# One layer of a streaming encoder: program order on every engine up to the MLP, the long convolution wholly on VectorE by a budget per weight unit, and w_out with twelve columns before the heads' rows

## The chip, the cores and the metric

One core of a Trainium2 chip runs the whole layer in one launch. The metric is the device time of an execution in microseconds (us), lower is better. TensorE (PE) multiplies, VectorE (DVE), ScalarE (ACT) and GpSimd (POOL) do the elementwise work, and the queue of SyncE (SP) issues nearly all transfers.

## What is computed

256 tokens of width 2048, float32. The layer is, cut to what matters:

```python
h = rms_norm(x, norm_mix_pre);  u = h @ w_in              # 2048 -> 4352 columns, split among three mixers
y_a = B * conv3(C * v)                                     # short convolution, 6 groups of 128 channels
y_b = silu(layer_norm(conv31(val * sigmoid(gate)) + bias)) # 6 heads of 128, norm over all 768 channels
y_c = (trailing_mean(u_c, {2,4,8,16}) - u_c) @ pool_w * pool_scale   # 4 groups of 128
x = x + rms_norm(concat(y_a, y_b, y_c) @ w_out, norm_mix_post)
h = rms_norm(x, norm_ffn_pre);  gate, val = split(conv3(h @ w_up) + bias)   # 2 x 5632 columns
x = x + rms_norm((silu(gate) * val) @ w_down, norm_ffn_post)
```

## The kernel before

**Units.** All four weight matrices lie in memory as one stream of units, each 128 partitions by 1024 floats (512 KB): units 0 to 67 are `w_in`, 68 to 99 `w_out`, 100 to 275 `w_up`, then `w_down`. A unit holds 8 blocks of 128 x 128. To reach float32 accuracy, every weight is split in a high and a low part: `load` (L97) brings `raw`, `split_hi` (L102) copies it rounded to `whi` on ScalarE, `split_lo` (L111) writes `wlo = raw - whi` on VectorE. There are 4 `raw` buffers and 5 of `whi` and `wlo`. The activations (`h1`, `y_t`, `h2`) are split the same way by `make_hi` (L332) and `make_lo` (L335). `product` (L244) runs three matmuls of 256 tokens for a block: `whi` with the high and the low activations, `wlo` with the high ones. So a unit is 24 matmuls. `ahead(u)` (L121) issues the splits up to unit u + 4 before the matmuls of unit u.

**First group.** `mm_group` (L284) takes the first 4 columns of `w_in` with 2 rows of blocks in a unit (units 0 to 7), while `start(k)` (L341) makes `h1` row by row from the loaded `xT` and squares it for the norm. GpSimd adds the squares.

**In-projection.** `mm_pair` (L276) makes two columns in 4 units, from unit 8 to 67: pairs for the 6 heads of mixer B (two of them in the first group), 2 pairs of pools, then `cv`, `cv`, `b` three times for mixer A. `evacuate` (L554) reads a finished pair from PSUM. For a head (`head_glu`, L390) it makes `glu`, and then the convolution with 31 taps: taps 2 to 22 are `tap` on VectorE (L404), in two sums `acc`; the last 8 (`POOL_TAPS`) are a ScalarE product `p` (L423) and a GpSimd add (L424) into `accp`, which GpSimd adds to `acc` at L427. The taps are closures in the list `background`. `between(kind)` pops 4 or 5 of them (`PACE`) in the middle and at the end of a pair. After the sixth head come the layer norm's closures: `mean`, six `centre`, `variance`, six `finish`. `later(n, f)` runs f some units later, at `tick`, after a unit's matmuls.

**w_out.** Its rows come in `OUT_ORDER`: pools, mixer A, then the heads (mixer B). The first 8 columns are one group, one row of blocks per unit (units 68 to 83). Before row 9 whatever is left of `background` is issued at once. Then the columns follow in pairs, the last pair (14, 15) in one PSUM tile `o14`; `out_tiles` (L591) squares and scales finished columns on ScalarE.

**The order on an engine.** Instructions of this part are issued through `nc.vector` and its like, and the framework's scheduler, which has its own time model, places them on each engine, except where `pin` keeps the program's order. `pinned` is False until the end of w_out, True from there to the norm of the MLP's input, and False again after it. Loads are pinned up to the end of the first group's section (L363). PSUM has 3 tiles of two banks (`banks`) and 2 small ones.

After w_out come a norm, `w_up` in pairs with a gate for each, `w_down` and the last norm.

## Time and profile before

| what | value |
|---|---|
| median of 3 runs | 1063.74 us (1062.91 to 1063.87) |
| the profiled execution | 1063.24 us |
| its span, first to last instruction | 1061.4 us |
| TensorE matmul busy | 1043.9 us, 98% of the span |
| VectorE, ScalarE, GpSimd busy | 730.0, 559.6, 194.3 us |
| granted TensorE clock, mean | 0.998 |
| read from memory | 194.57 MB, 185 GB/s over the span |

Busy time is time in which an engine executes; a wait of TensorE is a gap between its matmuls, put down to the instruction that ended it. Only gaps of the engine that sets the end cost anything. The first group runs to about 33 us, the in-projection to 213 us, w_out to 308 us, the MLP to the end.

### The profile page before, as it was taken

To read this page: it belongs to the slowest core of one execution; us is meant where nothing else is said; L and a number is where in the kernel's file an instruction comes from. 1 tells how busy PE (TensorE), PEld (TensorE's weight loads), DVE (VectorE), ACT (ScalarE), POOL (GpSimd) and SP (SyncE) were. 2 spreads that over 40 slices of the span, in tenths; PEclk is the share of its full clock that TensorE was granted. 3 is DMA by queue.
4 is the path that set the end of the run, shared out by engine and by line. 5 is a ranking of instruction groups with operands and counts; after the bars stand their busy time and mean duration, and the time that the engine had idled before them with its cause. 6 is when DMAs were issued, how large, how long until landed. Compare 5 with 4: busy or idle time off the path is not lost.

```text
span 1061.4 us, 16686 instructions
## 1 busy us (share of the span) xinstructions
PE 1043.9 (98%) x6485; PEld 932.1 (88%) x6485; DVE 730.0 (69%) x949; ACT 559.6 (53%) x781; POOL 194.3 (18%) x203
## 2 busy tenths in 40 slices
PE   8989999999999999999999999999999999999997
PEld 7989899999989988888888888888888888888886
DVE  7899988764448697786867868766766444454543
ACT  8645445556446575564655646655555343343431
POOL 4333556331114221110110101111111000000000
PEclk9999999999999999999999999999999999999999
DMA  8646466656645563765847648556556656565552
GB/s 278 221 139 193 156 188 201 202 174 186 193 139 178 181 192 124 233 204 151 251 153 225 213 133 261 188 192 191 186 186 232 188 189 195 183 193 184 195 180 80
DMA packets 73454, 199.85 MB, mean 188 GB/s; under 512 B 23712, under 2 KB 24608, under 8 KB 73248
## 3 DMA queue, kind: packets, MB, share of 16 engines
q1 hardware_dynamic: 72944, 197.39, 59.0%
q10 hardware_dynamic: 432, 1.40, 0.3%
q8 instruction: 51, 0.84, 0.3%
q14 instruction: 27, 0.22, 0.1%
HBM read 194.57 MB, written 2.10 MB: 185 GB/s over the span
## 4 chain that ended last, share of the span: by engine, by line
PE 89%; DVE 6%; issue 3%; DMA 1%; ACT 1%; SPq 0%; POOLq 0%; POOL 0%; DVEq 0%; ACTq 0%
PE gv L257 28%; PE gv L253 14%; PE o L247 9%; PE d L791 7%; PE d L793 7%; PE d L792 7%; PE in_cv L247 5%; PE up L247 4%; DVE acc L404 4%; PE in_b L247 3%; DVE wlo L115 1%; PE in L247 1%; DMA raw<-in_w_in 1%; PE in_head L247 1%; PE d3b L793 1%
## 5 line engine op out<-in xcount | busy, mean ns | idle before, releaser
L115 DVE TENSOR_TENSOR wlo<-raw,whi 128x1024 fp32r<-128x1024 f32 (+1 forms) x365 | 455.8, 1253 | 243.7 <-ACT whi L109 242.9
L109 ACT ACTIVATE whi<-raw 128x1024 fp32r<-128x1024 f32 (+1 forms) x365 | 383.9, 1055 | 334.5 <-PE d L793 103.1
L257 PE MATMUL gv<-h,whi 128*128 128x512 f32 x1280 | 443.2, 394 | 0.0
L253 PE MATMUL gv<-h,wlo 128*128 128x256 f32 x1280 | 346.3, 281 | 0.0
L257 PEld LDWEIGHTS gv<-h,whi 128*128 128x128 f32 x1280 | 234.9, 188 | 49.6
L253 PEld LDWEIGHTS gv<-h,wlo 128*128 128x128 f32 x1280 | 240.7, 188 | 6.8
L755 POOL TENSOR_TENSOR cg<-cg,cv 128x256 f32<-128x256 f32 x44 | 59.6, 1357 | 392.4 <-ACT cg L753 345.5
L791 PE MATMUL d<-whi,g_hi 128*128 128x512 f32 x308 | 121.7, 395 | 0.0
L793 PE MATMUL d<-whi,g_lo 128*128 128x512 f32 x308 | 121.2, 394 | 0.0
L792 PE MATMUL d<-wlo,g_hi 128*128 128x512 f32 x308 | 121.1, 393 | 0.0
L247 PE MATMUL o<-y_t,whi 128*128 128x256 f32 x512 | 91.5, 282 | 1.7 <-ACT yo L599 1.7
L247 PEld LDWEIGHTS o<-y_t,whi 128*128 128x128 f32 x512 | 78.5, 188 | 1.9 <-ACT yo L599 1.9
L247 PE MATMUL o<-y_t,wlo 128*128 128x256 f32 x256 | 72.0, 281 | 0.0
L793 PEld LDWEIGHTS d<-whi,g_lo 128*128 128x128 f32 x308 | 57.8, 188 | 13.9
L792 PEld LDWEIGHTS d<-wlo,g_hi 128*128 128x128 f32 x308 | 57.8, 188 | 13.6
L791 PEld LDWEIGHTS d<-whi,g_hi 128*128 128x128 f32 x308 | 57.8, 188 | 13.4
L247 PE MATMUL in_cv<-h,whi 128*128 128x256 f32 x384 | 68.9, 282 | 0.0
L404 DVE SCALAR_TENSOR_TENSOR acc<-glu,vec_sb,acc 128x246 f32<-128x246 f32 (+10 forms) x126 | 66.5, 567 | 2.5 <-POOL acc L427 2.2
L247 PEld LDWEIGHTS in_cv<-h,whi 128*128 128x128 f32 x384 | 59.0, 188 | 0.1
L247 PE MATMUL in_cv<-h,wlo 128*128 128x256 f32 x192 | 54.1, 282 | 1.1 <-DVE wlo L115 1.1
L749 ACT ACTIVATE u<-gv 128x512 f32<-128x512 f32 x40 | 23.7, 593 | 58.5 <-PE gv L257 58.5
L750 DVE TENSOR_TENSOR u<-gv,u 128x512 f32<-128x512 f32 x40 | 27.5, 688 | 37.8 <-ACT u L749 37.8
(155 smaller groups left out, 1275.2 us busy)
## 6 DMA issues: line engine op xcount, KB each, us to landing
raw<-in_w_up SPq DMA_DIRECT2D x176, 512.0 KB, 4.0
raw<-in_w_down SPq DMA_DIRECT2D x88, 512.0 KB, 3.5
raw<-in_w_in SPq DMA_DIRECT2D x67, 512.0 KB, 4.1
raw<-in_w_out SPq DMA_DIRECT2D x32, 512.0 KB, 4.1
xT<-blocks SPq DMA_DIRECT2D x64, 32.0 KB, 3.5
xT<-in_xt SPq DMA_DIRECT2D x7, 256.0 KB, 5.2
out<-tail_sb SPq DMA_DIRECT2D x6, 256.0 KB, 2.4
tail_sb<-in_g_row ACTq DMA_DIRECT2D x1, 1024.0 KB, 7.9
```

Of the source, the lines that this page charges most:

```text
L109: pin(nc.scalar.activation(hi[:, s], raws[i][:, s], AF.Copy))
L115: pin(nc.vector.tensor_tensor(lo[:, s], raw[:, s], hi[:, s].bitcast(F32), ALU.subtract))
L247: nc.tensor.matmul(ps, w, x, start=opens and n == 0, stop=last and n == 2, skip_group_check=True)
L253: pin(nc.tensor.matmul(ps[:, :T], w_lo, h[:, 0], start=False, stop=False))
L257: pin(nc.tensor.matmul(ps, w_hi, h, start=opens, stop=last))
L404: nc.vector.scalar_tensor_tensor(a[:, o:], glu[:, : T - o], cb(s), a[:, o:], ALU.mult, ALU.add)
L749: nc.scalar.activation(u, ps[:, :, T:], AF.Copy)
L750: nc.vector.tensor_tensor(u, ps[:, :, :T], u, ALU.add)
L755: nc.gpsimd.tensor_tensor(a, a, b, ALU.mult)
L791: nc.tensor.matmul(pss[h], g_hi[:, k, s], w1, start=(k == 0), stop=False)
L792: nc.tensor.matmul(pss[h], g_hi[:, k, s], w2, start=False, stop=False)
L793: nc.tensor.matmul(pss[h], g_lo[:, k, s], w1, start=False, stop=(k == KF - 1))
```

## The change

**Order.** `pinned` starts as True, and a wrapper `InOrder` pins whatever goes through `tensor`, `vector`, `scalar`, `gpsimd` in this part. Up to the MLP, every engine runs in the order in which the program issues. In the MLP the old `nc.` names remain.

**Start.** `step(n)` issues all of one unit's preparation: `make_hi`, `split_hi`, `make_lo`, `split_lo`, and the squares of the rows before. It runs four units ahead. Units 0 to 2 are split in halves and unit 1 is loaded in halves; row 1 of `xT` is loaded between the halves of unit 0; rows 8 to 13 no longer stand behind `raw` buffers in the queue, and unit 4's weights stand behind them.

**Budget.** `begin(u)` replaces `tick`, `between` and `PACE`. Ahead of the matmuls of unit u it runs what is due, then the splits (`ahead`), then the reading of a finished pair, then as many pieces of `background` as a credit allows: each unit adds 11.2 - 4.9 (in quarters of a microsecond), a tap costs 1.65, reading a pair 2.8 or 3.2, and so on.

**The convolution.** `POOL_TAPS` is gone: all taps from 2 to 30 of a head are VectorE instructions, 29 instead of 21. With them go the 48 ScalarE products, 42 GpSimd adds into `accp` and 6 GpSimd adds at L427. The head's sum for the norm is added when the head closes. Delays (`later`) are longer: 5 units to the mean's product, 3 to the variance's, 3 and 4 for the pools.

**w_out.** `OUT_TILES`: the ten rows of pools and mixer A for columns 0 to 7 and 8 to 11 (units 68 to 82), then the heads' six rows for 12 columns, 4 at a time (units 83 to 91), then columns 12 to 15 whole. Columns 14 and 15 have PSUM tiles of their own.

The number of matmuls, splits and loaded bytes is unchanged.

```diff
+FREE = 10
+OUT_TILES = (
+    [(k, m) for k in range(FREE) for m in range(8)]
+    + [(k, m) for k in range(FREE) for m in range(8, 12)]
+    + [(k, m) for g in (0, 4, 8) for k in range(FREE, KD) for m in range(g, g + 4)]
+    + [(k, m) for m in range(12, KD) for k in range(KD)]
+)
...
+SLOT, SPLIT, TAP = 11.2, 4.9, 1.65
+LOAD = {"head": 2.8, "pool": 3.2, "cv": 3.2, "b": 2.8}
...
     raws, parts = {}, {}
-    pinned, loading = [False], [True]
+    pinned, loading = [True], [True]
...
+    background, late, waiting = [], [], []
+    clock, closed, credit = [0], [False], [0.0]
+
+    def work(cost, fn):
+        background.append((cost, fn))
+
+    def later(n, fn, cost=0):
+        late.append((clock[0] + n, fn, cost))
+
+    def begin(u):
+
         clock[0] += 1
+        credit[0] = min(credit[0], TAP) + SLOT - SPLIT
         due = [e for e in late if e[0] <= clock[0]]
         for e in due:
             late.remove(e)
+            credit[0] -= e[2]
             e[1]()
+        ahead(u)
+        while waiting:
+            evacuate = waiting.pop(0)
+            credit[0] -= evacuate[0]
+            evacuate[1]()
+        while background and not closed[0] and credit[0] >= background[0][0]:
+            cost, fn = background.pop(0)
+            credit[0] -= cost
+            fn()
 
     def finish_background():
         while background or late:
-            run_background(len(background))
+            while background and not closed[0]:
+                background.pop(0)[1]()
             if late:
                 late.pop(0)[1]()
...
+    load(0, 2, lambda: load_x(1, 1))
     for c in range(1, 4):
         load_x(2 * c, 2)
-        load(c)
+        load(c, 2 if c == 1 else 1)
...
+        def step(n):
+
+            ks = (2 * n, 2 * n + 1)
+            if n:
+                for k in ks:
+                    make_hi(k, h1, "g_mix")
+                split_hi(n, 2 if n < 3 else 1)
+                for k in ks:
+                    make_lo(k, h1, "g_mix")
+                split_lo(n, 2 if n < 3 else 1)
+            else:
+                split_hi(0, 2, ahead=lambda j: make_hi(j, h1, "g_mix"))
+                split_lo(0, 2, ahead=lambda j: make_lo(j, h1, "g_mix"))
+            if 0 < n < 5:
+                load_x(2 * n + 6, 2)
+            for j in range(max(n - 1, 0), n + (n == KD // 2 - 1)):
+                square_sum(two(xT, j), sum_x, j == 0, f"sqx{j}")
+            done[0] = n + 1
...
+
+            def open_():
+                scalar.activation(
+                    acc[0], glu, AF.Identity, scale=cb(0), bias=v("cbb", i)
+                )
+                scalar.activation(acc[1], glu, AF.Copy, scale=cb(1))
 
...
-
-
-            ap = accp[:, i % 2]
-            base = K_B - POOL_TAPS
-
-            def pool_tap(s):
-                if s == base:
-                    nc.scalar.activation(ap, glu, AF.Copy, scale=cb(s))
-                    return
-                o = s - base
-                p = tmp(f"p{i}_{s}")
-                nc.scalar.activation(p[:, : T - o], glu[:, : T - o], AF.Copy, scale=cb(s))
-                nc.gpsimd.tensor_tensor(ap[:, o:], ap[:, o:], p[:, : T - o], ALU.add)
-
-            def pool_close():
-                nc.gpsimd.tensor_tensor(
-                    acc[1][:, base - 1 :], acc[1][:, base - 1 :], ap[:, : T - base + 1], ALU.add
-                )
-
-            def both(s):
-                tap(s)
-                if s - 2 < POOL_TAPS:
-                    pool_tap(base + s - 2)
-                if s - 2 == POOL_TAPS:
-                    pool_close()
-
-            for s in range(2, base):
-                background.append(lambda s=s: both(s))
-            background.append(close)
+                if i:
+                    a = heads[0][0] if i == 1 else totals[0]
+                    gpsimd.tensor_tensor(totals[0], a, acc[0], ALU.add)
+
             heads[i] = acc
+
+            def enqueue():
+                work(0, open_)
+                for s in range(2, K_B):
+                    work(TAP, lambda s=s: tap(s))
+                work(0, close)
+
+            later(1, enqueue)
...
             def mean():
-                for i in range(1, N_HEADS):
-                    a = acc[0] if i == 1 else tot[0]
-                    nc.gpsimd.tensor_tensor(tot[0], a, acc[i], ALU.add)
                 closed[0] = True
-                later(2, mean_product)
+                later(5, mean_product)
...
             def variance():
                 closed[0] = True
-                later(2, variance_product)
+                later(3, variance_product)
...
+        def wait_for(kind, i, ps):
+            waiting.append((LOAD[kind], lambda: evacuate(kind, i, ps)))
+
         u0 = 8
-        waiting = [(kind, i, ps) for (kind, i, _), ps in zip(IN_PAIRS, first)]
-
-        def scales_a():
-            stats["rx"] = token_rsqrt([sum_x], D, RMS_EPS, "x")
-
-        later(1, scales_a)
-        later(2, token_scales)
-
-        def between(kind):
-            while waiting:
-                evacuate(*waiting.pop(0))
-            run_background(PACE[kind])
-
+        for (kind, i, _), ps in zip(IN_PAIRS, first):
+            later(2, lambda kind=kind, i=i, ps=ps: evacuate(kind, i, ps), LOAD[kind])
         for kind, i, _ in IN_PAIRS[GROUP_IN // 2 :]:
-            ps = mm_pair(u0, f"in_{kind}{i}", h1, between=lambda: between(kind))
+            ps = mm_pair(u0, f"in_{kind}{i}", h1)
             u0 += 4
-            waiting.append((kind, i, ps))
-            between(kind)
+            wait_for(kind, i, ps)
...
-        def mixing(k):
-            if k == 9:
-                finish_background()
-            else:
-                run_background(4)
-
-        pss = mm_group(u0, "o", y_t, GROUP_OUT, mixing, OUT_ORDER)
-        u0 += 16
-        for n, ps in enumerate(pss):
-            out_tiles(2 * n, ps)
 
...
-        for m in range(GROUP_OUT, KD - 2, 2):
-            out_tiles(m, mm_pair(u0, f"o{m}", y_t, OUT_ORDER))
-            u0 += 4
-        ps = banks("o14")
-        mm_column(u0, ps[:, 0], y_t, OUT_ORDER)
-        out_tiles(KD - 2, ps[:, :1, :T], 1)
-        later(1, most_squares)
-        last = ps[:, 1, :T]
-        mm_column(u0 + 2, ps[:, 1], y_t, OUT_ORDER)
-        u0 += 4
-        pinned[0] = True
+
+        halves = {}
+
+        def out_bank(m):
+            if m in halves:
+                return
+            n = {0: 4, 4: 4, 8: 4, 12: 2, 14: 1, 15: 1}[m]
+            ps = banks(f"o{m}").rearrange("p b (j t) -> p (b j) t", j=2)
+            for j in range(n):
+                halves[m + j] = ps[:, j : j + 1]
+                if j % 2 == 0 and n > 1:
+                    halves[m + j, m + j + 1] = ps[:, j : j + 2]
+
+        for n in range(0, len(OUT_TILES), 8):
+            if OUT_TILES[n][0] == FREE:
+                finish_background()
+            begin(u0)
+            whi, wlo = parts.pop(u0)
+            for j, (k, m) in enumerate(OUT_TILES[n : n + 8]):
+                if k == 0 and m not in halves:
+                    out_bank(m)
+                c = slice(j * P, (j + 1) * P)
+                product(
+                    halves[m][:, 0], whi[:, c], wlo[:, c], y_t[:, OUT_ORDER[k]],
+                    k == 0 and (m % 2 == 0 or m == KD - 1), k == KD - 1,
+                )
+                if k == KD - 1 and m % 2 and m < KD - 2:
+                    later(1, lambda m=m: out_tiles(m - 1, halves[m - 1, m]))
+                elif k == KD - 1 and m == KD - 2:
+                    later(1, lambda m=m: out_tiles(m, halves[m], 1))
+                    later(2, most_squares)
+            u0 += 1
+        last = halves[KD - 1][:, 0]
```

**VectorE where the heads begin.** `vg0` and `vg1` are the two heads of the first group read from PSUM, `wlo13` to `wlo19` the low parts of units 13 to 19, `acc6` the taps. Before:

```order
L115 TENSOR_TENSOR wlo15_611<-raw15_608,whi15_610 128x1024
L404 SCALAR_TENSOR_TENSOR acc6_469<-glu6_468,vec_sb_71,acc6_469 128x254 x2
L392 TENSOR_TENSOR vg2_638<-in_head2_471,r_bc_544 128x512
L404 SCALAR_TENSOR_TENSOR acc6_469<-glu6_468,vec_sb_71,acc6_469 128x252 x2
L404 SCALAR_TENSOR_TENSOR acc6_469<-glu6_468,vec_sb_71,acc6_469 128x250 x2
L404 SCALAR_TENSOR_TENSOR acc6_469<-glu6_468,vec_sb_71,acc6_469 128x248 x2
L404 SCALAR_TENSOR_TENSOR acc6_469<-glu6_468,vec_sb_71,acc6_469 128x246
L404 SCALAR_TENSOR_TENSOR acc6_469<-glu6_468,vec_sb_71,acc6_469 128x254 x2
L404 SCALAR_TENSOR_TENSOR acc6_469<-glu6_468,vec_sb_71,acc6_469 128x244
L404 SCALAR_TENSOR_TENSOR acc6_469<-glu6_468,vec_sb_71,acc6_469 128x252 x2
L404 SCALAR_TENSOR_TENSOR acc6_469<-glu6_468,vec_sb_71,acc6_469 128x242
L115 TENSOR_TENSOR wlo16_663<-raw16_660,whi16_662 128x1024
```

Now:

```order
L112 TENSOR_TENSOR vg0_524<-in0_120,r_bc_520 128x512
L112 TENSOR_TENSOR vg1_528<-in0_120,r_bc_520 128x512
L146 TENSOR_TENSOR wlo13_535<-raw13_532,whi13_534 128x1024
L146 TENSOR_TENSOR wlo14_565<-raw14_562,whi14_564 128x1024
L112 SCALAR_TENSOR_TENSOR acc6_474<-glu6_473,vec_sb_71,acc6_474 128x254 x2
L112 SCALAR_TENSOR_TENSOR acc6_474<-glu6_473,vec_sb_71,acc6_474 128x252 x2
L146 TENSOR_TENSOR wlo15_601<-raw15_598,whi15_600 128x1024
L112 SCALAR_TENSOR_TENSOR acc6_474<-glu6_473,vec_sb_71,acc6_474 128x250 x2
L112 SCALAR_TENSOR_TENSOR acc6_474<-glu6_473,vec_sb_71,acc6_474 128x248 x2
L146 TENSOR_TENSOR wlo16_636<-raw16_633,whi16_635 128x1024
L112 TENSOR_TENSOR vg2_639<-in_head2_477,r_bc_520 128x512
L112 SCALAR_TENSOR_TENSOR acc6_474<-glu6_473,vec_sb_71,acc6_474 128x246 x2
```

Fifteen taps and the reading of the third head stood between `wlo15` and `wlo16`; now a unit's split is followed by four taps at most, and `vg2` is read after `wlo16`.

**The queue of loads at the start.** `xT` are rows of the input, `raw0` to `raw7` weight units. Before:

```order
L168 DMA xT_70<-in_xt 128x256
L100 DMA raw0_74<-in_w_in 128x512 x2
L168 DMA xT_70<-in_xt 128x256
L168 DMA xT_70<-in_xt 128x512
L100 DMA raw1_79<-in_w_in 128x1024
L168 DMA xT_70<-in_xt 128x512
L100 DMA raw2_82<-in_w_in 128x1024
L168 DMA xT_70<-in_xt 128x512
L100 DMA raw3_85<-in_w_in 128x1024
L100 DMA raw4_143<-in_w_in 128x1024
L168 DMA xT_70<-in_xt 128x512
L100 DMA raw5_181<-in_w_in 128x1024
```

Now:

```order
L210 DMA xT_70<-in_xt 128x256
L127 DMA raw0_74<-in_w_in 128x512
L210 DMA xT_70<-in_xt 128x256
L127 DMA raw0_74<-in_w_in 128x512
L210 DMA xT_70<-in_xt 128x512
L127 DMA raw1_79<-in_w_in 128x512 x2
L210 DMA xT_70<-in_xt 128x512
L127 DMA raw2_83<-in_w_in 128x1024
L210 DMA xT_70<-in_xt 128x512
L127 DMA raw3_86<-in_w_in 128x1024
L210 DMA xT_70<-in_xt 128x512 x3
L127 DMA raw4_171<-in_w_in 128x1024
```

The second half of `raw0` stands behind one more row of `xT`, `raw1` comes in halves at its old place, and three pieces of `xT` stand ahead of `raw4`.

**ScalarE at the end of w_out.** `sqy14` and `yo<-o14` read column 14, `whi102` is the split that needs the buffer freed by unit 97, the last unit of column 14; unit 98 is the first of column 15. Before:

```order
L109 ACTIVATE whi100_3679<-raw100_3677 128x1024
L595 ACTIVATE sqy12_3671<-o12_3550 128x512
L599 ACTIVATE yo_467<-o12_3550,vec_sb_71 128x256 x2
L109 ACTIVATE whi101_3709<-raw101_3707 128x1024
L109 ACTIVATE whi102_3743<-raw102_3741 128x1024
L595 ACTIVATE sqy14_3737<-o14_3676 128x256
L599 ACTIVATE yo_467<-o14_3676,vec_sb_71 128x256
```

Now:

```order
L138 ACTIVATE whi100_3591<-raw100_3589 128x1024
L138 ACTIVATE whi101_3622<-raw101_3620 128x1024
L112 ACTIVATE sqy14_3650<-o14_3595 128x256
L112 ACTIVATE yo_472<-o14_3595,vec_sb_71 128x256
L138 ACTIVATE whi102_3656<-raw102_3654 128x1024
```

The reading of column 14 stands ahead of `whi102`; column 15 is now written to a PSUM tile `o15`.

## Rows read from the trace of the kernel before

**Rows 1.** The page's busy times, engine by engine: busy us (share of the span) and instructions.

```profile
PE 1043.9 (98%) x6485; PEld 932.1 (88%) x6485; DVE 730.0 (69%) x949; ACT 559.6 (53%) x781; POOL 194.3 (18%) x203
```

**Rows 2.** Waits of TensorE over the whole execution: the waiting line and the one waited for, us in total, times, longest; without three waits outside this part or under 0.6 us.

```profile
PE in_head L247 <- DVE wlo L115: 3.3, 2, 2.3
PE o L247 <- ACT yo L599: 1.7, 1, 1.7
PE in L247 <- ACT whi L109: 1.5, 1, 1.5
PE pool L524 <- DVE pooled L517: 1.3, 2, 1.1
...
PE in_cv L247 <- DVE wlo L115: 1.1, 1, 1.1
...
PE in L247 <- DVE wlo L115: 0.7, 1, 0.7
PE in L247 <- DVE h L336: 0.7, 1, 0.7
```

**Rows 3.** Five stretches of the span: length, then busy time and instructions of PE, PEld (weight loads), DVE, ACT and POOL, then granted clock, DMA share, GB/s.

```profile
4.87:32.90 28.03, 25.11 (x196) 24.07 (x195) 24.77 (x27) 21.38 (x35) 10.82 (x7) 1.00 0.84 288
44.00:78.00 34.00, 30.69 (x257) 30.28 (x256) 33.99 (x50) 21.26 (x39) 17.00 (x19) 1.00 0.38 121
78.00:120.00 42.00, 39.82 (x331) 39.31 (x331) 42.00 (x69) 20.50 (x29) 18.50 (x18) 1.00 0.60 185
120.00:145.00 25.00, 24.78 (x206) 24.47 (x205) 25.00 (x45) 11.44 (x15) 8.71 (x10) 1.00 0.62 191
145.00:213.00 68.00, 68.00 (x577) 68.00 (x576) 56.27 (x72) 36.50 (x54) 36.96 (x33) 1.00 0.61 192
```

**Rows 4.** The chain that ended last, in order of time: start, length, what (x counts matmuls).

```profile
21.15 11.76 PE in L247 x95
32.90 2.85 PE in_head L247 x24
...
145.30 22.68 PE in_cv L247 x192
```

**Rows 5.** VectorE by line from 44 to 213 us: count, then busy us and mean ns of one, then idle time before them.

```profile
L115 DVE TENSOR_TENSOR wlo<-raw,whi 128x1024 fp32r<-128x1024 f32 x57 | 73.8, 1301 | 6.7 <-ACT whi L109 6.7
L404 DVE SCALAR_TENSOR_TENSOR acc<-glu,vec_sb,acc 128x246 f32<-128x246 f32 (+10 forms) x126 | 66.5, 567 | 2.5 <-POOL acc L427 2.2
L542 DVE SCALAR_TENSOR_TENSOR sa<-cv,vec_sb,sa 128x255 f32<-128x255 f32 (+1 forms) x12 | 9.1, 754 | 0.1
L392 DVE TENSOR_TENSOR vg<-in_head,r_bc 128x512 f32<-128x512 f32 x4 | 2.7, 676 | 0.0
L538 DVE TENSOR_TENSOR cv<-in_cv,cv 128x256 f32<-128x256 f32 x6 | 2.5, 417 | 0.1
```

**Rows 6.** GpSimd by line in the same stretch, same columns.

```profile
L424 POOL TENSOR_TENSOR accp<-accp,p 128x255 f32<-128x255 f32 (+6 forms) x42 | 42.0, 1000 | 25.6 <-ACT p L423 23.4
...
L427 POOL TENSOR_TENSOR acc<-acc,accp 128x234 f32<-128x234 f32 x6 | 7.1, 1180 | 3.7 <-DVE acc L404 3.5
```

**Rows 7.** VectorE in order of time, with runs of one line merged: start, length, line, shapes, count, idle time before.

```profile
28.48 0.87 DVE L336 SCALAR_TENSOR_TENSOR h<-xT,vec_sb,h 128x256 fp32r<-128x256 f32 x2
...
47.60 10.23 DVE L404 SCALAR_TENSOR_TENSOR acc<-glu,vec_sb,acc 128x252 f32<-128x252 f32 x13
57.75 1.64 DVE L115 TENSOR_TENSOR wlo<-raw,whi 128x1024 fp32r<-128x1024 f32 x1
...
60.85 1.22 DVE L115 TENSOR_TENSOR wlo<-raw,whi 128x1024 fp32r<-128x1024 f32 x1
61.98 1.62 DVE L404 SCALAR_TENSOR_TENSOR acc<-glu,vec_sb,acc 128x248 f32<-128x248 f32 x4
...
72.99 2.39 DVE L404 SCALAR_TENSOR_TENSOR acc<-glu,vec_sb,acc 128x252 f32<-128x252 f32 x6
```

**Rows 8.** All engines in order of time in the first 11 us, same columns.

```profile
3.06 0.43 SPq L100 DMA_DIRECT2D raw<-in_w_in  x1
...
3.82 0.63 ACT L109 ACTIVATE whi<-raw 128x512 fp32r<-128x512 f32 x1 [0.18 <-DMA raw<-in_w_in]
...
4.49 0.69 DVE L115 TENSOR_TENSOR wlo<-raw,whi 128x512 fp32r<-128x512 f32 x1 [0.33 <-ACT whi L109]
...
8.49 0.28 PE L247 MATMUL in<-h,wlo 128*128 128x256 f32 x1
9.18 1.06 ACT L109 ACTIVATE whi<-raw 128x1024 fp32r<-128x1024 f32 x1 [1.18 <-DMA raw<-in_w_in]
...
10.27 1.23 DVE L115 TENSOR_TENSOR wlo<-raw,whi 128x1024 fp32r<-128x1024 f32 x1 [2.28 <-ACT whi L109]
...
10.29 0.51 PE L247 MATMUL in<-h,whi 128*128 128x256 f32 x2 [1.52 <-ACT whi L109]
```

**Rows 9.** Transfers issued in the first 12 us: line, count, KB each, median us from issue to landing.

```profile
raw<-in_w_in SPq DMA_DIRECT2D x2, 256.0 KB, 3.0
```

**Rows 10.** All engines in order of time around column 14 of w_out, same columns as Rows 7.

```profile
299.80 1.06 ACT L109 ACTIVATE whi<-raw 128x1024 fp32r<-128x1024 f32 x1 [1.80 <-PE o L247]
...
301.03 0.47 ACT L599 ACTIVATE yo<-o,vec_sb 128x256 f32<-128x256 f32 x1
...
301.55 0.51 PE L247 MATMUL o<-y_t,whi 128*128 128x256 f32 x2 [1.67 <-ACT yo L599]
```

239 lines of the change are left out of this document (122 added, 117 removed).

## The prediction

> **What bounds the kernel now.** I read the busy times first, then TensorE's waits, then the stretches in which these lie, and last the order of time around each wait. TensorE's matmuls fill 98% of the span [rows 1], so a change that leaves the number of matmuls as it is can win only the gaps. The reader should take the size of the prize from the list of waits [rows 2]: 3.3 us before the heads' weights, 1.7 us before column 15 of w_out, 1.3 us before the pools' products, 1.1 us before a weight unit of `cv`, and 1.5 + 0.7 + 0.7 us in the first group; 10.3 us, about 1% of the time. Everything after w_out keeps its order on VectorE, and nothing there is touched.
>
> Why the gaps are there is read from the stretches [rows 3]. From 44 to 145 us VectorE is busy for 33.99 + 42.00 + 25.00 us of 101 and TensorE is not: the splits queue behind taps. At 47.60 us thirteen taps run for 10.23 us, and only then comes the low part of the unit that TensorE needs next [rows 7]. In the first group VectorE is busy for 24.77 of 28.03 us and TensorE stands still for 28.03 - 25.11 = 2.9 us [rows 3].
>
> The yardstick is a weight unit: 192 matmuls, 8 units, take 22.68 us [rows 4], 2.84 us for a unit. VectorE must not spend more than that on a unit on average.
>
> **The change part by part.** *Heads and pools.* The splits now stand at their unit, with at most four taps behind each, so the question is whether VectorE's work fits. I count the 60 units from 9 to 68 in the changed order, 60 x 2.84 = 170 us. There are 60 splits at 1.22 us [rows 7] = 73.2; 170 of the 174 taps at 2.39 / 6 = 0.40 us [rows 7] = 68.0; 9 readings of two columns at 0.68 [rows 5] = 6.1; about 40 instructions of 256 tokens at 0.42 [rows 5] and four tiny ones = 17.3. Sum 164.6 us. Back to back the next instruction starts earlier than the one before ends, at 61.98 us after a split that began at 60.85 and took 1.22 [rows 7], 0.09 us; for the 110 that are not taps (whose price has it already) that is 9.9 us less, 154.7.
>
> To this comes what GpSimd does to VectorE. A tap cost 0.567 us on average where it costs 0.40 when GpSimd rests [rows 5, 7]; splits 1.301 against 1.22, the `sa` taps 0.754 against 0.417. The excess is 126 x 0.167 + 57 x 0.081 + 12 x 0.337 = 29.7 us, while GpSimd was busy for 17.00 + 18.50 + 8.71 + 36.96 = 81.2 us [rows 3]: 0.37 us for each microsecond of GpSimd. The change removes 42.0 + 7.1 = 49.1 us of GpSimd [rows 6], so 32.1 remain and cost 11.7 us. VectorE then needs 166 us of 170. So the 48 taps that come back cost it 19.2 us, and GpSimd's silence gives nearly that back; a lag from a dense place is covered, since a split is issued four units ahead: 4 x 2.84 less 1.06 and 1.22 for its two halves [rows 7, 10] leaves 9 us. I take all of the 3.3 + 1.1 us as won; the bounds are none and all of it.
>
> The Trainium skill ("Perfetto Trace Analysis", section Optimizing Scalar/DVE Operations) would rather move work off a saturated VectorE to ScalarE or GpSimd, and warns that GpSimd shares a read port with it. By its first half the 19.2 us would lengthen the saturated stretch, to 1063.2 + 19.2 = 1082; the excess in the trace speaks for the second half.
>
> The pools' products wait for `pooled`, which stood between taps; now it is computed four units ahead of them, 11 us. The 1.3 us go; bounds as before.
>
> *Column 15.* ScalarE ran the split at 299.80 us first and read column 14 afterwards, to 301.50; TensorE began column 15 then [rows 10]. Columns 14 and 15 shared a tile. Now column 15 has its own, last used by columns 8 to 11, and the reading of 14 comes first. The 1.7 us go. What is late next is that split, issued four units ahead, with the 9 us above.
>
> *w_out.* Ten rows for 12 columns take 15 units where 10 rows for 8 columns took 10. The heads' rows are due 5 x 2.84 = 14 us later, which pays for the longer delays of the norm. No wait stood there before [rows 2], so I book nothing. If the cover is gone, the price is at most the three units in which the six heads arrive, 8.5 us.
>
> *First group.* `raw1` was issued at 3.06 us and used at 9.18 [rows 8]. Its first half stands at the same place with half of the bytes. The nearest rows are the halves of `raw0`, 3.0 us to landing [rows 9], and the whole `raw1`, 6.1; I take 5.0, between them and nearer to `raw1` because the transfers ahead are the same: 8.0 us. ScalarE's half split takes 0.63 and VectorE's 0.69 [rows 8], so VectorE begins its chain at 8.6 instead of 10.27. That chain, seven splits and twelve `make_lo`, ran without a pause to 28.48 + 0.87 = 29.35 us [rows 7]: 19.1 us. With 0.3 us for two splits in halves it now ends at 28.1, with unit 7's split as its last member. TensorE needs it 0.24 us into unit 7; a unit of the group takes 24 x 11.76 / 95 = 2.97 us [rows 4], so the group ends at 30.8 instead of 32.90: 2.1 us won. The upper bound is TensorE without any wait from 8.77 us, its first unit's end [rows 8]: 8.77 + 7 x 2.97 = 29.6, 3.3 us won. The lower bound is a loss of 1 us: unit 4's weights now stand behind three pieces of `xT`, 786 KB, 2.7 us at the 288 GB/s of this stretch [rows 3], and I count 1.7 us of spare time for them.
>
> *Sum.* 1063.24 (the profiled execution, span 1061.4 and 1.8 around it) - 3.3 - 1.1 - 1.3 - 1.7 - 2.1 = 1053.7. The median of the runs before lies 0.5 above its profiled execution; I add that: **1054.2 us**. Own range 1052 to 1056.5.
>
> **The rivals.** *VectorE becomes the bound (slower).* If the taps and GpSimd exclude each other wholly, each of the 32.1 us costs a full one, and if nothing of the overlap between instructions is left, VectorE needs 164.6 + 32.1 = 196.7 us for 170. Less the 9 us of lead, TensorE stands still for 17.6 us: 1054.2 + 17.6 = 1072. It costs more than the waits it removes from 0.75 us per microsecond of GpSimd on (164.6 + 0.75 x 32.1 = 170 + 9 + 9.5). For it: VectorE's lines were full for 101 us. Against it: the measured 0.37. The Trainium skill ("SBUF — State Buffer", section Who interferes with whom) states just that: a VectorE instruction with two inputs in SBUF and a GpSimd instruction that reads SBUF hold the shared port in turn, and the later one is fully blocked. The trace shows the contention but not the full price on VectorE's side; GpSimd can be the one that waits. Chance 0.07.
>
> *The first group does not gain.* Loads decide there, DMA is busy for 0.84 of the stretch [rows 3]: `raw1`'s first half lands hardly earlier, or `raw4` late. Then the time is 1054.2 + 2.1 = 1056.3, at the loss bound 1057.3. Chance 0.15.
>
> *The layer norm comes late.* In a fixed order each `finish` waits for ScalarE and GpSimd in turn, and unit 83 waits for it: up to 8.5 us, 1055 to 1062.7. Against it: the last of them is issued a unit before the first is needed, and the units 70 to 73 carry nothing but splits. Chance 0.08.
>
> *The waits only change places.* The order says what is issued, not when it runs; a fixed order can wait where the scheduler had found something else. If as much new waiting comes as went, the time is 1060 to 1064. Chance 0.08.
>
> **How the numbers follow.** Chances: forecast 0.62, rivals 0.07, 0.15, 0.08, 0.08. A measurement of this kernel tells 0.2%, 2.1 us, from no change. Faster by more: the forecast, the second rival and most of the third, 0.87. Within 0.2%: 0.07, from the third and fourth. Slower: 0.06, nearly all of the first. Range: the low end is the sum with 3.3 us at the start and the runs' spread, 1052; the high end 1060 takes in the second rival and most of the third, and leaves out the first, the fourth and a little below, 0.19.
>
> **What would show it.** Right: no wait of `in_head`, `in_cv` or `pool` matmuls over 0.5 us; the taps' mean near 0.44 us, 174 of them; column 15 begins without a gap; the first group ends near 30.8 us; the stretch from there to the end of w_out holds 92 units at 2.84 us. Wrong: waits for `wlo` in the units 20 to 68 (first rival), a gap before `in` matmuls released by `whi` and a DMA (second), a gap at the first heads' row in w_out (third).

## The result and the profile after

The changed kernel takes 1054.05 us (median of 4 runs, 1053.85 to 1054.36) where the kernel before, beside it on the same chip, takes 1063.80 (1062.91 to 1065.05): ratio 0.9908, 95% interval 0.9891 to 0.9925. The profiled execution takes 1054.36 us with a span of 1052.6, against 1063.24 and 1061.4: 8.8 us of the span to account for.

The page of the kernel after: the busy times that answer to [rows 1], and the line of the taps that answers to [rows 5] (count, busy us, mean ns of one).

```profile
PE 1042.4 (99%) x6485; PEld 930.9 (88%) x6485; DVE 733.5 (70%) x999; ACT 541.8 (51%) x735; POOL 140.5 (13%) x155
L112 DVE SCALAR_TENSOR_TENSOR acc<-glu,vec_sb,acc 128x254 f32<-128x254 f32 (+14 forms) x174 | 78.7, 507 | 0.0
```

All waits of TensorE of 0.2 us or more in the kernel after, without two that lie outside this part; the columns of [rows 2]. The waits of `in_head`, `in_cv`, `pool` and `o` are gone. What is left in this part lies in the first group: 2.8 us, about as much as before (1.5 + 0.7 + 0.7).

```profile
PE in L112 <- DVE wlo L146: 2.8, 5, 1.0
...
PE ss_y L112 <- ACT last_sq L687: 0.5, 1, 0.5
PE bc_x L112 <- POOL r_x L112: 0.2, 1, 0.2
```

To see where the 8.8 us lie, I cut both spans where TensorE's first matmul of a stage starts. The rows show the heads, `cv` and `b`, w_out up to the norm's product, and the pairs of `w_up`. Columns: stretch, length, TensorE's busy time and matmuls, granted clock, DMA share, GB/s. Before:

```profile
32.74:83.37 50.63, 47.32 (x398) 1.00 0.52 172
...
106.08:213.27 107.19, 104.79 (x875) 1.00 0.59 187
213.27:304.48 91.21, 89.54 (x756) 1.00 0.60 186
...
358.50:808.20 449.70, 449.70 (x2571) 1.00 0.62 192
```

After:

```profile
33.26:80.50 47.24, 47.04 (x398) 1.00 0.65 216
...
103.25:207.20 103.95, 103.95 (x874) 1.00 0.60 186
207.20:296.38 89.18, 89.18 (x756) 1.00 0.56 185
...
350.50:799.50 449.00, 449.00 (x2571) 1.00 0.62 192
```

The heads got 3.4 us shorter, `cv` and `b` with the pools' products 3.2, w_out 2.0, the MLP's pairs 0.7; the first group ends 0.5 us later (33.26 against 32.74, without a listed wait more), and the stretches not shown (pools, the norm, `w_up`'s group, `w_down`) differ by 0.1 at most. Sum: 0.5 - 3.4 - 3.2 - 2.0 - 0.7 = -8.8.

VectorE is the engine on which the forecast rested. Four stretches of the kernel after, columns of [rows 3]: it is busy for 158.5 of 163 us, 97%, and TensorE for all of them.

```profile
44.00:78.00 34.00, 34.00 (x290) 34.00 (x289) 31.92 (x58) 14.97 (x20) 3.34 (x4) 1.00 0.59 189
78.00:120.00 42.00, 42.00 (x353) 41.89 (x353) 41.02 (x71) 16.58 (x19) 11.47 (x17) 1.00 0.54 174
120.00:145.00 25.00, 25.00 (x210) 24.90 (x209) 24.22 (x42) 12.06 (x16) 3.83 (x4) 1.00 0.63 198
145.00:207.00 62.00, 62.00 (x526) 62.00 (x525) 61.29 (x107) 27.68 (x33) 5.99 (x7) 1.00 0.62 189
```

The first group, where the forecast expected 2.1 us and none came: VectorE and then GpSimd in the kernel after, in order of time (start, length, line, what, count, idle before).

```profile
8.99 1.33 DVE L146 TENSOR_TENSOR wlo<-raw,whi 128x512 fp32r<-128x512 f32 x2 [0.68 <-ACT whi L138]
10.79 0.89 DVE L374 SCALAR_TENSOR_TENSOR h<-xT,vec_sb,h 128x256 fp32r<-128x256 f32 x2 [0.47 <-ACT h L371]
...
18.22 1.21 DVE L146 TENSOR_TENSOR wlo<-raw,whi 128x1024 fp32r<-128x1024 f32 x1
19.36 3.02 DVE L374 SCALAR_TENSOR_TENSOR h<-xT,vec_sb,h 128x256 fp32r<-128x256 f32 x2
...
26.41 2.94 DVE L374 SCALAR_TENSOR_TENSOR h<-xT,vec_sb,h 128x256 fp32r<-128x256 f32 x2
29.27 4.62 DVE L146 TENSOR_TENSOR wlo<-raw,whi 128x1024 fp32r<-128x1024 f32 x4
```

```profile
18.54 2.04 POOL L112 TENSOR_TENSOR sum_x<-sum_x,sqx 128x512 f32<-128x512 f32 x1 [0.92 <-ACT sqx L363]
20.81 1.29 POOL L112 TENSOR_TENSOR sum_x<-sum_x,sqx 128x512 f32<-128x512 f32 x1 [0.22 <-ACT sqx L363]
...
25.34 3.72 POOL L112 TENSOR_TENSOR sum_x<-sum_x,sqx 128x512 f32<-128x512 f32 x2 [0.68 <-ACT sqx L363]
```

A pair of `make_lo` takes 0.89 us where GpSimd rests, and 2.94 to 3.02 us where two of GpSimd's additions of squares fall on the pair. Unit 7's split starts at 29.27 us and TensorE gets it at 30.5; the forecast had 28.1.

### The profile page after: what moved, and what is told of

Same layout as the page of the kernel before. It is cut to its first block, busy times and chain, and to the rows that moved or that the text cites. A ratio compares the mean times of both kernels' runs of the same rounds, so it can differ in the third digit from the quotient of the medians.

```text
span 1052.6 us, 16610 instructions
## 1 busy us (share of the span) xinstructions
PE 1042.4 (99%) x6485; PEld 930.9 (88%) x6485; DVE 733.5 (70%) x999; ACT 541.8 (51%) x735; POOL 140.5 (13%) x155
## 4 chain that ended last, share of the span: by engine, by line
PE 96%; DMA 1%; DVE 1%; issue 1%; ACT 1%; SPq 0%; POOL 0%; POOLq 0%; DVEq 0%; ACTq 0%
PE gv L112 43%; PE o L112 9%; PE d L847 7%; PE d L845 7%; PE d L846 7%; PE in_cv L112 6%; PE up L112 4%; PE in_head L112 4%; PE in_b L112 3%; PE in_pool L112 2%; DMA raw<-in_w_in 1%; PE d3b L847 1%; PE d3b L845 1%; PE d3b L846 1%; PE in L112 1%
## 5 line engine op out<-in xcount | busy, mean ns | idle before, releaser
L146 DVE TENSOR_TENSOR wlo<-raw,whi 128x1024 fp32r<-128x1024 f32 (+1 forms) x367 | 451.1, 1234 | 237.8 <-ACT whi L138 236.8
L112 DVE SCALAR_TENSOR_TENSOR acc<-glu,vec_sb,acc 128x254 f32<-128x254 f32 (+14 forms) x174 | 78.7, 507 | 0.0
L112 PE MATMUL o<-y_t,wlo 128*128 128x256 f32 x256 | 71.8, 281 | 0.0
L845 PEld LDWEIGHTS d<-whi,g_hi 128*128 128x128 f32 x308 | 57.8, 188 | 13.4
```

Of the source, the lines that this page charges most:

```text
L112: return lambda *a, **kw: pin(issue(*a, **kw))
L146: pin(nc.vector.tensor_tensor(lo[:, s], raw[:, s], hi[:, s].bitcast(F32), ALU.subtract))
L845: nc.tensor.matmul(pss[h], g_hi[:, k, s], w1, start=(k == 0), stop=False)
```

## The experiments

The changed kernel's ratio to the kernel before, 0.9908, is from a run of its own; the experiments below have, group by group, their own runs of the kernel before beside them. The intervals are about 0.15% to either side, so smaller differences between groups say nothing.

**e1: the GpSimd taps back in the new order**, `pool_tap` and `pool_close` as before. A tap's credit is 1.65 x 29 / 21 = 2.28, not the 2.19 of the expectation.

```diff
+            def both(s):
+                tap(s)
+                if s - 2 < POOL_TAPS:
+                    pool_tap(base + s - 2)
+                if s - 2 == POOL_TAPS + 4:
+                    pool_close()
...
-                for s in range(2, K_B):
-                    work(TAP, lambda s=s: tap(s))
+                for s in range(2, base):
+                    work(TAP * (K_B - 2) / (base - 2), lambda s=s: both(s))
```

> The changed kernel, with the last 8 taps of each head as a ScalarE product and a GpSimd add again, spread over the same units (21 VectorE taps a head at a credit of 2.19 each instead of 29 at 1.65). Theory A (the share-out per unit wins the waits, and what VectorE loses by 48 taps it gets back from GpSimd's silence, 0.37 us per microsecond of GpSimd): VectorE needs 164.6 - 9.9 - 19.2 + 0.37 x 81 = 165.5 us for units 9 to 68 instead of 166, so 1053.5 to 1056 us, taps' mean near 0.57 us, waits of TensorE before in_head and in_cv under 1 us together. Theory B (moving the taps wins the waits, the order alone does not): 3 to 6 us of waits before in_head, in_cv and in_b come back, 1057 to 1061 us. Theory C (GpSimd's price is higher than 0.37, as the taps' mean of 0.507 us with little GpSimd work hints): waits of 10 us or more, over 1063.

Measured: 1056.31 us (1055.38 to 1057.87), 0.9927 [0.9915, 0.9940]. No wait of `in_head` or `in_cv`, though GpSimd is busy for 71.8 us between 44 and 207 us where it was 24.6. VectorE by line there:

```profile
L147 DVE TENSOR_TENSOR wlo<-raw,whi 128x1024 fp32r<-128x1024 f32 x55 | 72.9, 1328 | 4.9 <-ACT whi L139 4.9
L113 DVE SCALAR_TENSOR_TENSOR acc<-glu,vec_sb,acc 128x254 f32<-128x254 f32 (+10 forms) x113 | 64.0, 608 | 6.0 <-POOL acc L113 6.0
```

The fixed order with its due times removes the heads' waits with the GpSimd taps too (theory A). What it costs is a wait of 1.4 us of `ln_mean` for GpSimd's sum. In the fixed order the move of the taps is worth some 2 us of the 9.8 (0.9927 against 0.9908; the intervals overlap). It also prices GpSimd: over the whole span VectorE is busy for 731.3 us here and 733.5 in the change, so the 48 taps, 19.2 us at 0.40, cost it 2.2 net; 17.0 us came back for 190.9 - 140.5 = 50.4 us less of GpSimd, 0.34 us for each.

**e2: the scheduler again.** `pinned = [False]` up to the end of w_out, the rest as changed.

> The changed kernel, with the framework's scheduler placing the instructions up to the end of w_out again (pinned False there), everything else as in the change. It puts up to eight taps between two splits where the changed order has four at most. Theory A (the fixed order keeps each split at its unit and so wins the waits): 1 to 4.5 us of waits for wlo come back between 44 and 145 us, 1055 to 1059 us. Theory B (the tap budget as the program issues it is enough, the scheduler would keep to it): 1053.5 to 1054.8 us, no such waits over 0.5 us.

Measured: 1066.15 us (1064.68 to 1066.98), 1.0022 [1.0013, 1.0031]: slower than before. From 44 to 120 us TensorE never waits, so neither theory holds: the order does matter, but elsewhere. The longest waits of TensorE:

```profile
PE in L112 <- DVE wlo L146: 6.4, 5, 4.5
PE pool L112 <- DVE pooled L112: 4.0, 1, 4.0
```

VectorE in the first group, in order of time:

```profile
16.68 6.58 DVE L374 SCALAR_TENSOR_TENSOR h<-xT,vec_sb,h 128x256 fp32r<-128x256 f32 x6
```

The scheduler put six `make_lo` ahead of a split that TensorE stood for (4.5 us), and the pools' `pooled` far behind the taps (4.0 us). Without GpSimd's taps the heads do not need the fixed order; the pools and the start do.

**e3: w_out with 8 columns.**

```diff
-    [(k, m) for k in range(FREE) for m in range(8)]
-    + [(k, m) for k in range(FREE) for m in range(8, 12)]
-    + [(k, m) for g in (0, 4, 8) for k in range(FREE, KD) for m in range(g, g + 4)]
-    + [(k, m) for m in range(12, KD) for k in range(KD)]
+    [(k, m) for k in range(KD) for m in range(8)]
+    + [(k, m) for m in range(8, KD) for k in range(KD)]
...
-            n = {0: 4, 4: 4, 8: 4, 12: 2, 14: 1, 15: 1}[m]
+            n = {0: 4, 4: 4, 8: 2, 10: 2, 12: 2, 14: 1, 15: 1}[m]
```

> The changed kernel, with w_out as 8 columns in one group and then single columns, so that the heads' rows are due 5 units earlier, at unit 78, and the layer norm's last steps are issued there at once. Theory A (the 12 columns pay for the longer delays of the norm): at unit 78 TensorE waits for bc_ln, a VectorE multiplication, Silu, the high part and the low part one after the other, 2.5 to 4 us: 1056.5 to 1058 us. Theory B (the norm had time to spare, the tiling is worth nothing): under 0.5 us, 1054 us. If everything that stands ahead at that unit piles up, up to 8.5 us.

Measured: 1059.71 us (1058.32 to 1060.32), 0.9957 [0.9945, 0.9970], 5.7 us more than the change. The waits are as theory A has them, 1.1 + 1.6 us; the rest is the clock. TensorE in order of time without its plain matmuls, and then the stretch (columns as in the cut by stages):

```profile
237.57 0.71 PE L110 MATMUL bc_ln<-ident,r_ln 128*128 128x128 f32 x4 [1.09 <-POOL r_ln L110]
239.87 1.04 PE L110 MATMUL o<-y_t,whi 128*128 128x256 f32 x2 [1.59 <-ACT y_t L110]
```

```profile
237.00:247.00 10.00, 7.84 (x40) 0.66 0.27 99
```

Over these 10 us, which begin with the waits, the granted clock is 0.66 of 2.4 GHz, a mix of its two levels (1.2 and 2.4 GHz): the upper level would have had room for 3.4 us more. So a row of waits of 2.7 us cost 5.7. Two of the five runs, with a mean granted clock of 0.998 instead of 0.995, took 1058.32 and 1059.05 us, nearer to the waits alone.

**e4: the first group without six of GpSimd's seven additions** (the sum of squares over the rows is left out).

```diff
-            if not first:
+            if name == "sqx7":
                 gpsimd.tensor_tensor(total, total, sq, ALU.add)
```

> The changed kernel without six of the seven GpSimd additions of the squares in the first group (the sum over the row pairs is left out, so the first norm's scale is not the reference's). Theory A (the pairs of make_lo, 1.7 to 3.0 us beside an addition where they take 0.87 alone, made VectorE's chain end at 30.5 instead of 28.1 us): pairs take 0.9 us, the last split of the group ends near 27, TensorE leaves the group near 30.3 to 31 instead of 33.3 us, and the time is 2 to 3 us less, 1051 to 1052. Theory B (the transfers decide, raw4 and its like come late): the gaps before the low parts are filled by gaps before whi and a DMA, less than 0.8 us won, 1053.3 to 1054.3.

Measured: 1051.74 us (1051.08 to 1052.66), 0.9885 [0.9872, 0.9899]. VectorE in order of time, and the row of TensorE that ends the group:

```profile
18.77 0.87 DVE L374 SCALAR_TENSOR_TENSOR h<-xT,vec_sb,h 128x256 fp32r<-128x256 f32 x2
...
24.43 1.23 DVE L146 TENSOR_TENSOR wlo<-raw,whi 128x1024 fp32r<-128x1024 f32 x1 [0.25 <-ACT whi L138]
```

```profile
30.15 0.95 PE L112 MATMUL ss_x<-ones,sum_x 128*128 128x1 f32 x8
```

Each pair takes 0.87 us, unit 7's split starts at 24.43 instead of 29.27, and the group ends at 30.15 instead of 33.26 (theory A). Of the 3.1 us, 1.5 go to a new wait for `bc_x`: `m_x` stands on VectorE behind unit 11's split, whose weights have not landed. `make_lo` as a whole falls from 14.2 us of busy time to 7.1.

**e5: columns 14 and 15 in one tile again**, in different banks of it; the reading of 14 stays ahead of the split.

```diff
-            n = {0: 4, 4: 4, 8: 4, 12: 2, 14: 1, 15: 1}[m]
+            n = {0: 4, 4: 4, 8: 4, 12: 2, 14: 2}[m]
...
-                halves[m + j] = ps[:, j : j + 1]
-                if j % 2 == 0 and n > 1:
+                at = 2 * j if m == 14 else j
+                halves[m + j] = ps[:, at : at + 1]
+                if j % 2 == 0 and n > 1 and m < 14:
```

> The changed kernel with columns 14 and 15 of w_out in one PSUM tile again (different banks of it); the reading of column 14 stays ahead of the split of unit 102. Theory A (the tile of its own is what frees column 15): TensorE waits at unit 98 for the reading of column 14, which with nothing ahead of it takes a square and a scaling on ScalarE, 0.4 + 0.47 us and the way there: 0.9 to 1.3 us more, 1055 to 1055.4. Theory B (the reading ahead of the split was enough): under 0.3 us, 1054.1. Theory C (tiles do not matter and the 1.7 us went elsewhere): no wait at all.

Measured: 1055.13 us (1054.72 to 1055.81), 0.9920 [0.9905, 0.9934], and one wait more than the change has:

```profile
PE o L112 <- ACT yo L112: 0.9, 1, 0.9
```

Theory A, by the wait; the time alone (0.9920 against 0.9908) would not tell. Of the 1.7 us the tile of its own removes 0.9; the other 0.8 go with the split that no longer runs ahead of the reading, which was not undone by itself.

**e6: the kernel before in the program's order**, `pinned = [True]` and nothing else.

> The kernel before, with every instruction up to the end of w_out kept in the program's order and nothing else changed: its four or five taps between two pairs of splits, its GpSimd taps, its w_out. Theory A (the fixed order by itself wins the waits of the in-projection): no waits of in_head and in_cv over 0.5 us, 4 to 5 us less than before up to unit 67, so 1058 to 1060 us if nothing new waits. Theory B (a fixed order needs the due times and the budget): where the scheduler had found something else, VectorE or TensorE now stands for GpSimd (pools, layer norm before row 9 of w_out), 3 us or more of new waits, 1062 to 1070 us.

Measured: 1088.74 us (1087.99 to 1089.73), 1.0235 [1.0220, 1.0251]. Theory B, and far beyond its range. Its two longest waits of TensorE:

```profile
PE ln_mean L100 <- POOL lnt L100: 9.6, 1, 9.6
PE in L100 <- ACT h L100: 6.5, 1, 6.5
...
```

The product `ln_mean` is asked for where it is written down, and in the fixed order TensorE stands there until GpSimd's sum is made; the other wait is one of the first group. In the change, which asks for products at due times, neither exists. The change differs from e6 in its start, budget and w_out as well, so the share of the due times alone is not shown.

**e7: the squares added later**, meant to be faster than the change.

```diff
-                sq = mixt.tile([P, 512], F32, tag="sq", name=name)
-            pin(nc.scalar.activation(sq, src, AF.Square))
-            if not first:
-                gpsimd.tensor_tensor(total, total, sq, ALU.add)
+            pin(nc.scalar.activation(two(yo, int(name[3:])), src, AF.Square))
...
+        def add_squares(js):
+            for j in js:
+                a = two(yo, 0) if j == 1 else sum_x
+                vector.tensor_tensor(sum_x, a, two(yo, j), ALU.add)
...
+            if k == 8:
+                add_squares(range(1, 8))
...
-                later(3, lambda: token_scales())
+                later(4, lambda: token_scales())
```

On VectorE the additions stand behind unit 7's split. The first heads are read one unit later, and `SLOT` is 11.4.

> The changed kernel, with the seven additions of the first group's squares on VectorE behind the group's last split, instead of on GpSimd beside make_lo (the squares stand in yo until then); the reading of the first two heads one unit later and a credit of 11.4 instead of 11.2 per unit to make up for it. Nothing is left out. Theory A (GpSimd's additions lengthened make_lo): the group ends near 30.2 us as without additions, unit 8's split ends at 31.2 just in time, and the 1.5 us wait for bc_x seen without additions is gone: 1050.5 to 1052 us. Theory B (the work is only moved): VectorE's 4.2 us of additions make units 8 and 9 wait, or the convolution ends later and the heads' rows come late: 1053 to 1057.

Measured: 1051.26 us (1051.18 to 1051.47), 0.9883 [0.9868, 0.9898], the fastest of those that leave nothing out. VectorE, and TensorE's waits in the group:

```profile
25.19 0.68 DVE L112 TENSOR_TENSOR sum_x<-yo 128x512 f32<-128x512 f32 x1
25.91 4.46 DVE L112 TENSOR_TENSOR sum_x<-sum_x,yo 128x512 f32<-128x512 f32 x6
30.28 4.62 DVE L146 TENSOR_TENSOR wlo<-raw,whi 128x1024 fp32r<-128x1024 f32 x4
```

```profile
PE ss_x L112 <- DVE sum_x L112: 0.6, 1, 0.6
...
PE in L112 <- DVE wlo L146: 0.5, 2, 0.2
```

Theory A: the additions cost VectorE 5.1 us at a place where TensorE waits 0.6 us for their sum, and the 2.8 us of waits become 1.1. Three things change at once here; which share each has is not shown.

**e8: 48 more GpSimd additions**, one at each of the units 16 to 63, 128x256, from and into rows of `yo` (`extra[0]`) that are not in use yet.

```diff
+        if 16 <= u < 64:
+            y = extra[0]
+            gpsimd.tensor_tensor(y[:, 0], y[:, 1], y[:, 2], ALU.add)
...
+        extra.append(yo)
+        gpsimd.memset(yo[:, 1:3], 0.0)
```

> The changed kernel with one more GpSimd addition of 128x256 (both operands in SBUF, no one waits for the result) at each of the units 16 to 63, 48 in all, about 0.8 us each or 38 us. It prices what GpSimd costs VectorE. By 0.37 us per microsecond VectorE loses 14 us, which the lead of four units covers in great part: 1054 to 1060, taps' mean 0.55 to 0.6 us. By the 0.78 that the changed kernel's own rows give (20 us of excess for 26 us of GpSimd): 30 us, of which some 20 are not covered, 1070 to 1080. By full exclusion: 38 us, 1080 to 1090.

Measured: 1075.02 us (1074.22 to 1077.78), 1.0103 [1.0086, 1.0120]. Over the whole span GpSimd is busy for 188.6 us instead of 140.5, VectorE for 755.4 instead of 733.5: 21.9 / 48.1 = 0.46 us for each microsecond of GpSimd. The time is that of the second theory, the price lies between the first two. VectorE by line (44 to 207 us) and waits of TensorE:

```profile
L112 DVE SCALAR_TENSOR_TENSOR acc<-glu,vec_sb,acc 128x254 f32<-128x254 f32 (+14 forms) x143 | 78.5, 601 | 0.0
```

```profile
PE in_cv L112 <- DVE wlo L146: 7.5, 7, 2.2
PE ln_mean L112 <- POOL lnt L112: 4.1, 1, 4.1
```

With VectorE at 97% there was no room for 21.9 us. TensorE's new waits for VectorE (`in_cv` and `in_b` for `wlo`, `pool` for `pooled`) come to 10.7 us; the 4.1 us of `ln_mean` are GpSimd's own lateness, and the mean granted clock falls from 0.999 to 0.992. So a VectorE that runs out of time is real, at 0.46 us and not at the full exclusion of the first rival; the change stays clear of it because it takes GpSimd work away.

**e9 and e10: the budget paid out at every fourth, every second unit** (`EVERY` 4 and 2): 14, and 7 or 8, taps in a row.

```diff
+EVERY = 4
...
-        credit[0] = min(credit[0], TAP) + SLOT - SPLIT
+        credit[0] = min(credit[0], TAP + (EVERY - 1) * (SLOT - SPLIT)) + SLOT - SPLIT
...
-        while background and not closed[0] and credit[0] >= background[0][0]:
+        while (
+            (u % EVERY == 0 or u > 66)
+            and background and not closed[0] and credit[0] >= background[0][0]
+        ):
```

> The changed kernel with the same budget paid out at every fourth unit: 14 taps in a row after one split, then three units with splits alone, up to unit 66. Theory A (the share per unit is what keeps TensorE fed): 14 taps take 14 x 0.507 = 7.1 us where 3.75 took 1.9, so the splits behind come 5.2 us later; the rows of the changed kernel show splits done some 5 to 6 us ahead of need among the heads and 2 to 4 us around the pools and the first cv, so the waits come there, 1 to 3 us each at three or four places: 1057 to 1064. Theory B (four units of lead cover any bunch of this size, due work ahead of the splits is enough): under 0.5 us, 1053.8 to 1054.6.

> The same at every second unit: seven or eight taps in a row, as many as the scheduler put between two splits of the changed kernel. Theory A: the splits behind come 1.8 us later than in the change, less than their lead everywhere: under 0.5 us of waits, 1053.8 to 1054.8. Theory B (any bunch costs): 1 to 3 us, 1055 to 1057.

Measured: e9 1054.46 us (1054.41 to 1054.77), 0.9916 [0.9902, 0.9929]; e10 1054.58 us (1054.21 to 1055.00), 0.9917 [0.9904, 0.9931]. No wait of TensorE for a split after the first group in e9: theory A falls for e9, and e10 bears out its own theory A, which expected less than 0.5 us of waits. Sharing the taps out unit by unit is worth nothing that can be measured while GpSimd is silent; four units of lead carry 14 of them. The stretch of one bunch in e9 (columns of [rows 3]), and the bunch:

```profile
50.09:55.69 5.60, 5.60 (x50) 5.60 (x49) 5.59 (x15) 3.33 (x4) 0.29 (x1) 1.00 0.34 119
```

```profile
50.09 5.60 DVE L113 SCALAR_TENSOR_TENSOR acc<-glu,vec_sb,acc 128x254 f32<-128x254 f32 x14 [0.98 <-ACT acc L113]
```

And the same cut of the kernel before around its 13 taps of [rows 7]:

```profile
47.60:57.83 10.23, 9.59 (x82) 9.38 (x80) 10.23 (x15) 10.22 (x20) 9.56 (x13) 1.00 0.05 19
```

14 taps take 5.60 us with GpSimd silent (0.29 us busy), 13 took 10.23 us with GpSimd busy for 9.56. ScalarE was full as well, with nine products, four splits and other work; but the first of these splits was done at 50.6 us, and its low part, the one that TensorE waited for, came only when the taps ended, at 57.75. So the heads' wait came from the bunch on VectorE. VectorE made no low part in it, so no `raw` buffer came free, and the DMA share fell to 0.05. The bunch was long because of GpSimd, not because of the count of its taps: in e8 additions on GpSimd alone raise the taps' mean from 0.507 to 0.601 us. The next run takes both GpSimd's and ScalarE's part of the taps away.

**e11: the kernel before without GpSimd taps.**

```diff
-POOL_TAPS = 8
-PACE = {"head": 5, "pool": 4, "cv": 4, "b": 5}
+POOL_TAPS = 0
+PACE = {"head": 7, "pool": 5, "cv": 5, "b": 7}
...
...
-                if s - 2 == POOL_TAPS:
+                if POOL_TAPS and s - 2 == POOL_TAPS:
...
-                run_background(4)
+                run_background(6)
```

> The kernel before, scheduler, w_out and all, with the last 8 taps of each head on VectorE as well and 7, 5, 5, 7 instead of 5, 4, 4, 5 closures at a time. In the kernel before 13 taps beside GpSimd took 10.23 us, GpSimd busy for 9.56 of them, and ScalarE was full with products; 14 taps in a row in the changed kernel took 5.60 us with GpSimd silent. Theory A (GpSimd's and ScalarE's part of the taps made the bunch long, and so the heads wait): no wait of in_head over 0.5 us, the stretch from the first group's end to the pools 3 us shorter than before; what the scheduler does to the pools' products and to column 15 stays: 1058 to 1062 us. Theory B (the scheduler puts splits late whatever the taps cost): in_head waits 2 us or more as before, and 48 more taps on VectorE make it 1064 to 1070.

Measured: 1062.78 us (1062.43 to 1063.81), 0.9993 [0.9984, 1.0002]. Its waits of TensorE of 1 us or more up to the end of w_out, but for the warm-up, then two stretches (columns as in the cut by stages):

```profile
PE pool L524 <- DVE pooled L517: 4.5, 2, 2.3
PE o L247 <- ACT yo L599: 1.7, 1, 1.7
```

```profile
140.00:145.00 5.00, 2.70 (x8) 0.76 0.69 203
145.00:150.00 5.00, 5.00 (x41) 0.90 0.54 164
```

The waits of `in_head` (3.3 us) and `in_cv` (1.1 us) are gone with the scheduler still at work, and from the heads' first matmul to the pools' it takes 47.6 us instead of 50.7: theory A for the mechanism. The gain is spent again at the pools, where `pooled` comes later than before (4.5 us instead of 1.3) and the granted clock falls with it; that is why the time, 1062.78, is a little above its range, and why moving the taps alone gains nothing that can be measured (0.9993).

## Why the prediction was right, and where its steps were not

- **Heads and `cv` (3.3 + 1.1 us): right in size, not in the whole reason.** Two things in the change each remove these waits: the taps' move (e11, e2) and the fixed order with due times (e1). The forecast saw the reason in splits that "stand at their unit, with at most four taps behind each"; e9 shows that with GpSimd silent the evenness does nothing. VectorE's budget came out as forecast, 97% of the time (166 of 170 us there, 158.5 of 163 here).
- **The price of GpSimd: right.** The forecast took 0.37 us per microsecond; the same work taken away is worth 0.34 (e1), and added work at a full VectorE costs 0.46 (e8). "The taps' mean near 0.44 us" compared two different numbers: the mean of one (0.507) counts the overlap of neighbours, the busy time does not, and 78.7 / 174 = 0.45 us is what answers to the 0.40 taken from six taps in a row. The 0.37 has the same mixture in it, with 0.567 less 0.40.
- **Pools' products (1.3 us): right, and the fixed order with its due times is what wins them.** With the scheduler and as many VectorE taps the wait is 4.0 to 4.5 us (e2, e11), and a fixed order without due times left 4.4 (e6).
- **Column 15 (1.7 us): right**; 0.9 by the tile, the rest by the order on ScalarE (e5). The stretch got 2.0 us shorter.
- **w_out, booked at nothing: right.** The 12 columns do cover the norm's delays; without them it costs 5.7 us (e3), within the forecast's price of up to 8.5, but the clock, about half of it, was not among its reasons.
- **First group (2.1 us): wrong, the second rival's case by another cause.** `raw1`'s first half was used at 8.33 us (8.0 forecast) and VectorE began at 8.99 (8.6), so the start was close. The step that failed is the length of VectorE's chain: it "ran without a pause" for 19.1 us before, and with 0.3 us more for the halves "it now ends at 28.1". It took 21.5 us and ended at 30.5. Of the 2.4 us, 0.4 are the later start; 1.0 are two pauses for ScalarE (0.47 and 0.53 us); and some 0.8 are GpSimd's additions, whose part in the chain the forecast took over as it was. Before, the first of the seven, at 8.08 us, fell ahead of the chain, and the other six lengthened it by 6.3 us. In the new order they start at 13.30, all seven fall on the chain, and lengthen it by 7.1. e4 and e7 show what a chain without them is worth: 2.3 to 2.8 us.
- **What made up for it.** The stretch of `cv` and `b` got 3.2 us shorter where 2.4 were waits, w_out 2.0 where 1.7 were, and the MLP's pairs 0.7 where none was forecast: 1.8 us in which the kernel before lists no wait. 0.7 of this lies at the pools' products. Before, they come in four pairs with other matmuls between them; the three units around them took 13.4 us, which is three units at 2.84, the waits of 2.4 and 2.5 us more. After, they come four in a row; the four units took 13.2, four at 2.84 and 1.8 more. The first products, before and after:

```profile
117.96 0.70 PE L524 MATMUL pool<-pooled,pw_sb 128*128 128x256 f32 x2 [1.11 <-DVE pooled L517]
...
118.96 0.59 PE L524 MATMUL pool<-pooled,pw_sb 128*128 128x256 f32 x2
...
111.81 1.03 PE L112 MATMUL pool<-pooled,pw_sb 128*128 128x256 f32 x4
```

The MLP's 0.7 (0.6 from first matmul to first matmul) goes with the code of the two kernels: 449.6 us in the three that keep the program of before (e6, e11 and itself), 449.0 in the changed one and the nine made from it. It is spread evenly over the stage. Its cause stays open, and so does that of the remaining 0.4 us.

From profile to profile the forecast says 9.5 us and the trace 8.9: at the first group 2.6 us are missing (2.1 forecast as won, 0.5 lost), and 1.8 us came unforeseen. So the number came out better than its sum, in part by luck. The median is nearer still (1054.2 forecast, 1054.05 measured) because the forecast added 0.5 us for a median above its profiled run; after the change the median lies 0.3 below it.

The Trainium skill ("SBUF — State Buffer", section Who interferes with whom) holds that the order of issue, not the shape of the operation, decides whether VectorE or GpSimd blocks. The first group agrees: the split at 18.22 us, under way when the addition starts at 18.54, keeps its 1.21 us while the addition takes 2.04 instead of 1.29, and the pair behind the split, which meets a second addition as well, takes 3.02 us instead of 0.87. A split in that place is lengthened too. In the kernel before, the second of two splits, behind the start of an addition at 17.19 us, took 2.31 us (VectorE, then GpSimd):

```profile
16.22 3.44 DVE L115 TENSOR_TENSOR wlo<-raw,whi 128x1024 fp32r<-128x1024 f32 x2
...
17.19 1.39 POOL L327 TENSOR_TENSOR sum_x<-sum_x,sqx 128x512 f32<-128x512 f32 x1 [1.57 <-ACT sqx L325]
```

In e8 the 48 additions took 0.99 us each, 47.7 us, and cost VectorE 21.9 us; how long they waited themselves no run here shows.

## What to carry to other kernels

Before work is moved between two engines, cut the trace to the few microseconds in which the wait arises and read the other engines' busy time there: thirteen taps cost 0.79 us each in that place and 0.40 elsewhere, which no mean over the stage shows. A fixed program order paid here, together with a due time for every asked-for product; on the code written for a scheduler it cost 25 us. In a chain that ends a stage, the additions whose sum is not needed yet can be the ones to move.
